# Block 2's attention as a pipeline of query tiles with a fixed TensorE order, its values in two passes, and nine of 62 filter taps taken off VectorE

## The chip, the cores and the metric

The kernel runs on 1 core of one Trainium2 chip. The metric is the device time of one execution in microseconds (us). A core has five engines that run at the same time, each through its own list of instructions in order: TensorE (PE in the profile; its weight loads are PEld), VectorE (DVE), ScalarE (ACT), GpSimd (POOL) and SyncE (SP), which here only issues DMAs.

## The reference, cut to what matters

Two transformer blocks run one after the other on a sequence of 512 tokens of width 1024, in float32. The change is inside the mixer of the second block, which sends four column groups of one projection `u = h @ w_in` through four mixers and joins them:

```python
z = val * jax.nn.sigmoid(gate)                       # conformer mixer: 256 channels
z = causal_depthwise_conv(z, dw_w) + dw_b            # 31 taps per channel
z = group_norm_channels(z, gn_g, gn_b)               # mean and variance over 64 channels
y_a = jax.nn.silu(z)
y_b = b_gate * causal_depthwise_conv(c_gate * xs, conv_w)        # short mixer, 3 taps
y_c = moba_attention(u_att)                          # 4 heads of 64, 512 keys
y_d = h_lru * jax.nn.gelu(gate)                      # RG-LRU: two small products, gates, a scan
y = jnp.concatenate([y_a, y_b, y_c, y_d], axis=-1) @ w_out[l]
```

With 512 tokens the attention is an ordinary causal softmax with a linear distance bias, four heads of width 64: scores, softmax over the keys, and the product with the values.

## The kernel before, in words

The sequence is four token tiles of 128 (`NT = 4`). A product in nearly full float32 precision is made of three passes of a faster type (`F32R`): each operand is split into a high part, copied by ScalarE, and a low part, `source - high`, by VectorE (`split`, L111 to L113), and `mm3` adds high x high, high x low and low x high in one PSUM bank. A weight column block of 1024 rows x 128 columns is eight such triples, 24 matmuls into one tile `cm` of 128 channels x 512 tokens (`cm_phase`, L156). Weights come by SP's DMA queue into `rawc`/`rawr`, and ScalarE and VectorE split them into `wh` and `wl`, five buffers of each (`WB = 5`).

The program is written for a tile framework that schedules it: each engine's order is set by the framework's own timeline, not by the order of the Python code alone. So in the kernel before, matmuls of the attention and of the projections may change places on TensorE.

Block 2's mixer, in the order of the code. First the conformer's gate and value blocks give `zp` (a padded 128 x 542 tile for each half of the 256 channels). The filter is 62 VectorE steps, 31 for each half, into `cacc0` and `cacc1` (`taps`, L1125): one `tensor_scalar` and 30 `scalar_tensor_tensor` each. They wait in a list `bg`, and `pump(n)` takes the next n of them into the program at chosen places, `RATE = 5` behind each column block. Then come the attention's query and key blocks (`aq_evac`, `ak_evac`), and the value block in token layout (`tm_block`, tile `tmc`, evacuated to `av` in plain float32).

Then the four heads follow one after another. `at_head(h)` makes four query tiles of scores (`as`, two passes), adds the bias and takes the row minimum on VectorE (L1192, tile `aL`), the exponential with its row sum on ScalarE (L1194), the reciprocal and the scaling on VectorE (L1195, L1196), and the transposes on TensorE (`apt`, L1199), which ScalarE and VectorE copy in turn to `apts` (L1200). Four float32 value products follow (`ao`, L1250). Behind each head come two or three of nine more column blocks (`rest`: gate, RG-LRU input, short mixer), and behind the first two heads one half of the RG-LRU (`lru`, tiles `lps`, `xc`). Behind head 2 all remaining taps are put in and the group norm begins (`conf_mean`, tile `cmu`); behind head 3 it ends (`conf_norm`, tile `cva`).

PSUM has eight banks: three for `cm`, `lps`, `cmu` and `cva` in rotation (`mm`), two for scores (`s`), two for transposes (`pt`), one for the value product (`o`). The output projection of the mixer follows (`tm_phase` with `order4 = [6, 7, 2, 3, 4, 5, 0, 1]`, tile `tm`, L223 to L227): it takes the RG-LRU's chunks first, then the short mixer's (2, 3), the attention's (4, 5) and the conformer's (0, 1).

Of the kernel before, what the change touches and what calls it, by code (L numbers as in the profile page):

```python
# [8 lines left out]
F32 = mybir.dt.float32  # L9
F32R = mybir.dt.float32r  # L10
AF = mybir.ActivationFunctionType
OP = mybir.AluOpType
# [3 lines left out]
P = 128  # L16
T = 512
NT = T // P
D = 1024
KC = D // P  # L20
# [6 lines left out]
NEG = -1.0e30  # L27
# [14 lines left out]
def tile_two_blocks(ctx: ExitStack, tc: tile.TileContext, a: dict, out: bass.AP, dbg=None):  # L42
# [39 lines left out]
    ident = consts.tile([P, P], F32, name="ident")  # L82
# [69 lines left out]
    def pump(n):  # L152
        for _ in range(min(n, len(bg))):
            bg.pop(0)()
# [881 lines left out]
    for g in range(2):  # L1036
        pool.memset(gmean[64 * g:64 * g + 64, 64 * g:64 * g + 64], 1.0 / 64.0)
    def tmp():
        return mx.tile([P, T], F32, name="tmp", tag="tmp", bufs=6)

    zp = [mx.tile([P, 30 + T], F32, name=f"zp{c}") for c in range(2)]
    th_g = {}
# [38 lines left out]
    cs, cx = {}, {}  # L1081

    def sc_c(c):
        def f(ps):
            cs[c], cx[c] = tmp(), tmp()
            act.activation(cs[c], ps, AF.Copy)
        return f

    def sc_x(c):
        def f(ps):  # L1090
            dve.tensor_mul(cx[c], cs[c], ps)
            w = pv[:, c, SCW:SCW + 3]
            act.activation(cs[c], cx[c], AF.Copy, scale=w[:, 2:3])
            for j in (1, 0):
                s = 2 - j
                dve.scalar_tensor_tensor(cs[c][:, s:], cx[c][:, :T - s], w[:, j:j + 1], cs[c][:, s:],
                                         op0=OP.mult, op1=OP.add)
        return f

    def sc_b(c):  # L1100
        def f(ps):
            dve.tensor_mul(cx[c], cs[c], ps)
            split(H3[0][:, 2 + c, :], H3[1][:, 2 + c, :], cx[c])
        return f

    gl = {}
# [15 lines left out]
    lg = col_blocks(w_in2, 2304, 256)  # L1122
    acc = [mx.tile([P, T], F32, name=f"cacc{c}") for c in range(2)]

    def taps(c):  # L1125
        z, w = zp[c], half[:, c, :]
        bg.append(lambda: dve.tensor_scalar(acc[c], z[:, 0:T], w[:, 0:1], pv[:, c, DWB:DWB + 1],
                                            op0=OP.mult, op1=OP.add))
        for j in range(1, 31):
            bg.append(lambda j=j: dve.scalar_tensor_tensor(acc[c], z[:, j:j + T], w[:, j:j + 1], acc[c],  # L1130
                                                           op0=OP.mult, op1=OP.add))

    sq, var = {}, {}

    def conf_mean():
        for c in (1, 0):
# [45 lines left out]
    def at_head(h):  # L1182
        pts = m2.tile([P, NT, T], F32, name="apts", tag="apts", bufs=1)
        for i in range(NT):
            n = (i + 1) * P
            s = psm.tile([P, T], F32, name="as", tag="s", bufs=2)
            m = max(n, 256)
            for j in range(2):
                pe.matmul(s[:, :m], aq(h)[:, i * P:(i + 1) * P], ak(h)[j][:, :m], start=j == 0, stop=j == 1)
            L = m2.tile([P, T], F32, name="aL", tag="aL", bufs=2)  # L1190
            st = m2.tile([P, 3], F32, name="ast", tag="ast", bufs=4)
            dve.tensor_tensor_reduce(L[:, :n], s[:, :n], ab[:, T - n:], scale=-0.25 ** (h + 1), scalar=-NEG,  # L1192
                                     op0=OP.add, op1=OP.min, accum_out=st[:, 0:1])
            act.activation(L[:, :n], L[:, :n], AF.Exp, scale=-1.0, bias=st[:, 0:1], accum_out=st[:, 1:2])  # L1194
            dve.reciprocal(st[:, 2:3], st[:, 1:2])  # L1195
            dve.tensor_scalar(L[:, :n], L[:, :n], st[:, 2:3], None, op0=OP.mult)  # L1196
            pt = psm.tile([P, NT, P], F32, name="apt", tag="pt", bufs=2)
            for kb in range(i + 1):
                pe.transpose(pt[:, kb, :], L[:, kb * P:(kb + 1) * P], ident)  # L1199
            (act.copy if i % 2 else dve.tensor_copy)(pts[:, 0:i + 1, i * P:(i + 1) * P], pt[:, 0:i + 1, :])  # L1200
        return pts
# [4 lines left out]
    for c in (1, 0):  # L1206
        taps(c)
    dump("x3", X)
    lnp.release()
    psm = Banks(mm=(0, 1, 2), s=(3, 4), pt=(5, 6), o=(7,))  # L1210
# [10 lines left out]
    akp = m2.tile([P, 2, 2, T], F32R, name="akp")  # L1221

    def aq(h):
        return H3[h % 2][:, 4 + h // 2, :]

    def ak(h):
        return [H3[i][:, h, :] if h < 2 else akp[:, h - 2, i, :] for i in range(2)]

    av = m2.tile([P, NT, 256], F32, name="av")
# [8 lines left out]
    rest = chunks[5:]  # L1238
    for c in range(2):
        rest += [(sc[c], sc_c(c)), (sx[c], sc_x(c)), (sb[c], sc_b(c))]  # L1240
    cuts = (0, 3, 4, 6, len(rest))


    for c in range(2):
        o = psm.tile([P, T], F32, name="ao", tag="o", bufs=1)
        for e in range(2):
            h = 2 * c + e
            pts = at_head(h)
            for kb in range(NT):
                pe.matmul(o[64 * e:64 * e + 64, kb * P:], av[:, kb, h * 64:(h + 1) * 64], pts[:, kb, kb * P:],  # L1250
                          start=kb == 0, stop=kb == NT - 1)
            cm_phase(*MM, rest[cuts[h]:cuts[h + 1]], X3, 0, rate=RATE)
            if h in (0, 1):
                lru(h)
            if h == 2:
                pump(len(bg))
                conf_mean()
            if h == 3:
                conf_norm()
        split(H3[0][:, 4 + c, :], H3[1][:, 4 + c, :], o)  # L1260
    dump("h3h", H3[0].bitcast(F32))
    m2.release()
    mx.release()
# [145 lines left out]
```

## Time and profile before

| | before |
|---|---|
| median of 3 runs | 1320.06 us (1317.81 to 1320.11) |
| the profiled execution, its own time | 1320.28 us |
| its span, first to last instruction | 1318.6 us |
| mean granted TensorE clock | 0.994 |
| TensorE busy | 1302.3 us, 99% |
| VectorE busy | 744.4 us, 56% |
| ScalarE busy | 533.9 us, 40% |
| GpSimd busy | 75.8 us, 6% |

The profiled execution's own time lies 0.2 us above the median, and 1.7 us of it lie outside the span. The mixer's part that the change touches runs from about 785 to 925 us of the span. Times in rows are counted from the span's start. A matmul's listed duration includes its way through the array, so the time that one takes from the next is read from start to start.

### The profile page before, as it was taken

What the parts mean: (1) busy time and instruction counts of PE and PEld (TensorE: products, weight loads), DVE (VectorE), ACT (ScalarE), POOL (GpSimd) and SP (SyncE); (2) the same over time, 40 slices, a digit from 0 to 9 for tenths busy, and PEclk for the clock granted to TensorE, in tenths of its full rate; (3) what the DMA queues carried; (4) which work ended last, traced back from release to release, by engine and by line L of the source; (5) the groups of instructions that cost most, each with busy time, mean ns of one, the idle gap of its engine ahead of it and who ended that gap; (6) DMA issues with size and microseconds to landing.
All of it is one profiled execution on the core that took longest, in us unless ns stands there. A gap on an engine that the chain in (4) does not pass through costs nothing.

```text
span 1318.6 us, 17034 instructions
## 1 busy us (share of the span) xinstructions
PE 1302.3 (99%) x6906; PEld 1115.0 (85%) x6906; DVE 744.4 (56%) x1203; ACT 533.9 (40%) x893; POOL 75.8 (6%) x152
## 2 busy tenths in 40 slices
PE   9999999999999999999999999999999999999998
PEld 8899899899889888888888898767898888888886
DVE  6764876574666655556633569985553334532432
ACT  5764564333423433344432134665433223431321
POOL 3220020110010000000000120000100000000000
PEclk9999999998999999999999999989999999999999
DMA  8322344522223342323233024212324332223211
GB/s 267 97 67 71 112 138 158 200 90 99 94 96 130 111 128 65 127 68 124 82 110 128 32 69 147 73 37 64 99 95 128 96 96 97 96 96 112 96 37 59
DMA packets 92148, 134.87 MB, mean 102 GB/s; under 512 B 4572, under 2 KB 77329, under 8 KB 92062
## 3 DMA queue, kind: packets, MB, share of 16 engines
q1 hardware_dynamic: 88446, 128.53, 29.9%
q10 hardware_dynamic: 2968, 3.14, 0.7%
q0 software_dynamic: 656, 2.12, 0.5%
q8 instruction: 54, 0.88, 0.3%
q14 instruction: 24, 0.20, 0.0%
HBM read 131.66 MB, written 2.12 MB: 101 GB/s over the span
## 4 chain that ended last, share of the span: by engine, by line
PE 94%; DVE 3%; ACT 2%; issue 0%; DMA 0%; POOL 0%; ACTq 0%; DVEq 0%; POOLq 0%
PE cm L139 15%; PE cm L138 15%; PE cm L140 15%; PE tm L227 9%; PE tm L223 9%; PE tm L224 9%; PE tmc L200 2%; PE tmc L201 2%; PE tmc L199 2%; PE tr L294 1%; PE tm L138 1%; PE tm L140 1%; PE tm L139 1%; PE num L687 1%; DVE cacc L1130 1%; PE mls L667 1%
## 5 line engine op out<-in xcount | busy, mean ns | idle before, releaser
L113 DVE TENSOR_TENSOR wl<-rawc,wh 128x1024 fp32r<-128x1024 f32 x140 | 170.7, 1222 | 203.2 <-ACT wh L112 202.9
L112 ACT ACTIVATE wh<-rawc 128x1024 fp32r<-128x1024 f32 x140 | 147.7, 1058 | 224.9 <-PE cm L139 190.6
L113 DVE TENSOR_TENSOR wl<-rawr,wh 128x1024 fp32r<-128x1024 f32 x73 | 88.9, 1223 | 147.1 <-ACT wh L112 147.1
L112 ACT ACTIVATE wh<-rawr 128x1024 fp32r<-128x1024 f32 x73 | 76.9, 1060 | 174.6 <-PE tm L227 126.5
L139 PE MATMUL cm<-x2l,wh 128*128 128x512 f32 (+1 forms) x392 | 143.8, 368 | 0.0
L140 PE MATMUL cm<-x2h,wl 128*128 128x512 f32 (+1 forms) x392 | 143.7, 367 | 0.0
L138 PE MATMUL cm<-x2h,wh 128*128 128x512 f32 (+1 forms) x392 | 143.1, 368 | 0.0
L139 PE MATMUL cm<-x4l,wh 128*128 128x512 f32 (+1 forms) x296 | 106.6, 361 | 1.3 <-DVE x4l L113 1.3
L140 PE MATMUL cm<-x4h,wl 128*128 128x512 f32 (+1 forms) x296 | 106.4, 360 | 0.0
L138 PE MATMUL cm<-x4h,wh 128*128 128x512 f32 (+1 forms) x296 | 106.1, 361 | 0.1
L139 PEld LDWEIGHTS cm<-x2l,wh 128*128 128x128 f32 x392 | 73.9, 189 | 12.2
L140 PEld LDWEIGHTS cm<-x2h,wl 128*128 128x128 f32 x392 | 73.8, 189 | 12.1
L138 PEld LDWEIGHTS cm<-x2h,wh 128*128 128x128 f32 x392 | 73.6, 189 | 12.2
L631 DVE SCALAR_TENSOR_TENSOR uy<-cm,fw,uy 128x511 f32<-128x511 f32 x88 | 65.5, 747 | 1.4
L138 PE MATMUL cm<-x3h,wh 128*128 128x512 f32 (+1 forms) x184 | 64.2, 354 | 0.8 <-DVE xc L631 0.6
L139 PE MATMUL cm<-x3l,wh 128*128 128x512 f32 (+1 forms) x184 | 64.5, 351 | 0.0
L139 PEld LDWEIGHTS cm<-x4l,wh 128*128 128x128 f32 x296 | 55.8, 189 | 9.8 <-DVE x4l L113 1.5
L140 PE MATMUL cm<-x3h,wl 128*128 128x512 f32 (+1 forms) x184 | 63.9, 349 | 0.0
L138 PEld LDWEIGHTS cm<-x4h,wh 128*128 128x128 f32 x296 | 55.5, 189 | 8.9 <-DVE x4l L113 0.3
L140 PEld LDWEIGHTS cm<-x4h,wl 128*128 128x128 f32 x296 | 55.8, 189 | 8.5
L329 POOL TENSOR_TENSOR rs_r<-rs_e,mhalf 128x1 f32<-128x1 f32 (+1 forms) x16 | 24.2, 1510 | 540.6 <-DVE rs_e L328 540.6
L200 PE MATMUL tmc<-wl,xh 128*128 128x256 f32 (+1 forms) x160 | 46.5, 290 | 0.7 <-DVE wl L113 0.7
(460 smaller groups left out, 3053.1 us busy)
## 6 DMA issues: line engine op xcount, KB each, us to landing
rawc<-in_ffn_w_up_dram SPq DMA_DIRECT2D x22, 1024.0 KB
rawc<-in_w_in_dram SPq DMA_DIRECT2D x20, 1024.0 KB
rawc<-in_mlp_w_dram SPq DMA_DIRECT2D x16, 1024.0 KB
rawr<-in_mlp_w_dram SPq DMA_DIRECT2D x16, 1024.0 KB
rawr<-in_ffn_w_down_dram SPq DMA_DIRECT2D x11, 1024.0 KB
rawr<-in_w_out_dram SPq DMA_DIRECT2D x10, 1024.0 KB
rawc<-in_xa_wkv_dram SPq DMA_DIRECT2D x8, 1024.0 KB
rawc<-in_xa_wq_dram SPq DMA_DIRECT2D x4, 1024.0 KB
```

What stands on the lines that cost most here:

```text
L112: act.activation(hi, src, AF.Copy)
L113: dve.tensor_sub(lo, src, hi.bitcast(F32))
L138: pe.matmul(ps, wh, xh, start=first, stop=False)
L139: pe.matmul(ps, wh, xl, start=False, stop=False)
L140: pe.matmul(ps, wl, xh, start=False, stop=last)
L199: pe.matmul(o, xh, wh, start=k == 0, stop=False)
L200: pe.matmul(o, xh, wl, start=False, stop=False)
L201: pe.matmul(o, xl, wh, start=False, stop=k == KC - 1)
L223: pe.matmul(ps[t][h], xh, wh[:, c], start=i == 0, stop=False)
L224: pe.matmul(ps[t][h], xh, wl[:, c], start=False, stop=False)
L227: pe.matmul(ps[t][h], xl, wh[:, c], start=False, stop=i == n - 1)
L631: dve.scalar_tensor_tensor(dst[:, s:], ps[:, :T - s], w[:, j:j + 1], y[:, s:], op0=OP.mult, op1=OP.add)
```

## The change

Six things change, all in block 2's mixer.

1. The attention runs as one pipeline over 16 units (four heads x four query tiles). Step u issues the scores of unit u, then 12 or 15 matmuls of the nine column blocks (a generator, `stream`), then the transposes of unit u - 2, and in every second step the value product of a pair of query tiles, whose second tile was transposed one step before.
2. These matmuls and transposes are wrapped in `in_order`, which keeps them on TensorE in the order of the code. The other engines are still scheduled by the framework.
3. The values are split (`av`: 64 high and 64 low columns side by side), the transposed probabilities are split too (`ptp`), and the value product is two passes of 256 columns per key block; the high and low output halves are added afterwards (`aos`). The scaling by the reciprocal sum goes from VectorE to ScalarE.
4. Of the second half's 31 taps, nine go to ScalarE: the first writes `cacc1`, eight write a scaled copy `ctap` (two buffers), and a DMA on GpSimd's queue adds each to `cacc1`. They are spaced by `next_act_tap` at nine places. VectorE's 22 other taps of that half start when the last add has landed.
5. The background list holds all of half 0, then half 1, and is taken out 4 steps behind a query or key block, 6 behind a half of the value block, then 1 or 2 in each step of the pipeline.
6. One square in `lru` goes from VectorE to ScalarE, the order of the two halves in the group norm changes, and it stands behind the whole attention.

```diff
+    in_order = tc.keep_in_program_order
...
-    def taps(c):
-        z, w = zp[c], half[:, c, :]
-        bg.append(lambda: dve.tensor_scalar(acc[c], z[:, 0:T], w[:, 0:1], pv[:, c, DWB:DWB + 1],
-                                            op0=OP.mult, op1=OP.add))
-        for j in range(1, 31):
...
+    NDMA = 8
+
+    def act_tap(j):
+        z, w = zp[1], half[:, 1, :]
+        if j == 0:
+            act.activation(acc[1], z[:, 0:T], AF.Identity, scale=w[:, 0:1], bias=pv[:, 1, DWB:DWB + 1])
+            return
+        t = mx.tile([P, T], F32, name="ctap", tag="ctap", bufs=2)
+        in_order(act.activation(t, z[:, j:j + T], AF.Copy, scale=w[:, j:j + 1]))
+        pool.dma_start(acc[1], t, accum_op=OP.add)
...
+            for j in range(NDMA + 1 if c else 1, 31):
+                bg.append(lambda z=z, w=w, c=c, j=j: dve.scalar_tensor_tensor(
+                    acc[c], z[:, j:j + T], w[:, j:j + 1], acc[c], op0=OP.mult, op1=OP.add))
...
-        dve.tensor_mul(lps[0], av_, av_)
+        act.activation(lps[0], av_, AF.Square)
...
-        act.activation(av[:, t0:t0 + 2, :], ps.rearrange("p (u c) -> p u c", u=2), AF.Copy)
+        v = av[:, t0:t0 + 2].rearrange("p u h d -> p (u h) d")
+        split(v[:, :, 0:64], v[:, :, 64:P], ps.rearrange("p (u d) -> p u d", d=64))
         pump(RATE)
+        next_act_tap()
-    RATE = 5
+    RATE = 6
...
-    cm_phase(*MM, ATT, X3, 0, rate=RATE)
+    for chunk in ATT:
+        cm_phase(*MM, [chunk], X3, 0, rate=4)
+        next_act_tap()
...
+    def stream():
+        for n, (src, evac) in enumerate(rest):
+            w = split_w(src())
+            ps = psm.tile([P, T], F32, name="cm", tag="mm", bufs=3)
+            for k in range(KC):
+                for i, (wi, xi) in enumerate(((0, 0), (0, 1), (1, 0))):
+                    in_order(pe.matmul(ps, w[wi][:, k, :], X3[xi][:, k, :], start=k == 0 and i == 0,
+                                       stop=k == KC - 1 and i == 2))
+                if k == KC - 1:
+                    evac(ps)
+                if (n, k) in ((2, KC - 1), (3, 5)):
+                    lru(n - 2)
+                yield
...
-            dve.tensor_scalar(L[:, :n], L[:, :n], st[:, 2:3], None, op0=OP.mult)
+        act.activation(L[:, :n], L[:, :n], AF.Copy, scale=st[:, 2:3])
...
+        d = ptp[i // 2][:, :, 0:i + 1, (i % 2) * P:(i % 2 + 1) * P]
+        split(d[:, 0], d[:, 1], pt[:, 0:i + 1, :])
...
+        for kb in range(2 * p + 2):
+            for i in range(2):
+                in_order(pe.matmul(o[:, p * 256:(p + 1) * 256], av[:, kb, h, :], ptp[p][:, i, kb, :],
+                                   start=kb == 0 and i == 0, stop=kb == 2 * p + 1 and i == 1))
...
+    for u in range(N + 3):
+        if u < N:
+            at_scores(*units[u])
+        upto = min((u + 1) * len(rest) * KC // N, len(rest) * KC)
+        for _ in range(upto - done):
+            next(filler)
+        done = upto
+        if 2 <= u < N + 2:
+            at_turn(*units[u - 2])
+        if u >= 4 and u % 2 == 0:
+            at_sum(units[u - 3][0], units[u - 3][1] // 2)
+        if u in (0, 2):
+            next_act_tap()
+        pump(1 if u < 3 else 2)
```

What this does to the lists of instructions is seen at two places. On TensorE in the kernel before, around the first value product (`ao`), the rows are these; `cm` is a column block, `apt` a transpose, `as` a score, `lps` a product of the RG-LRU:

```order
L1199 MATMUL apt<-ident,aL 128x128 x4
L1189 MATMUL as<-h3h,h3l 128x256
L1189 MATMUL as<-h3l 128x256
L1189 MATMUL as<-h3h,h3l 128x256
L1189 MATMUL as<-h3l 128x256
L1250 MATMUL ao<-apts,av 64x512
L1250 MATMUL ao<-apts,av 64x384
L1250 MATMUL ao<-apts,av 64x256
L1250 MATMUL ao<-apts,av 64x128
L1189 MATMUL as<-h3h,h3l 128x384
...
L1163 MATMUL lps<-xc_6842,bd 128x512 x2
L1199 MATMUL apt<-ident,aL 128x128 x3
```

On TensorE now, at its first value product (the first pair of query tiles of head 0), with the rows of the next step behind it:

```order
L1258 MATMUL cm<-x3h,wl 128x512
L1291 MATMUL apt<-ident,aL 128x128 x3
L1301 MATMUL ao<-apts_7471,av 128x256 x4
L1277 MATMUL as<-h3h,h3l 128x256
L1277 MATMUL as<-h3l 128x256
L1258 MATMUL cm<-x3h,wh 128x512
...
L1188 MATMUL lps<-xc_6842,bd 128x512 x2
...
L1291 MATMUL apt<-ident,aL 128x128 x4
```

Before, the value products stood among scores and transposes, in four sizes; now each stands behind 12 column-block matmuls and one unit's transposes, and no later matmul of the pipeline may pass it.

On VectorE now, from the first unit's transposes (`apt_7560`) to the second's (`apt_7601`); `cacc1` is the second filter half, whose first VectorE tap this is, and L115 is the low part of a split:

```order
L115 TENSOR_TENSOR apts0_7471<-apt_7560,apts0_7471 128x128
L1283 RECIPROCAL ast_7572<-ast_7572 128x1
L115 TENSOR_TENSOR wl_7902<-rawc_7778,wh_7901 128x1024
L1155 SCALAR_TENSOR_TENSOR cacc1_6845<-zp1_6839,half_628,cacc1_6845 128x512
L1280 ISA aL_7611,ast_7612<-as_7608,ab_7158 128x128
L1280 ISA ast_7612 128x1
L633 SCALAR_TENSOR_TENSOR xc0_6842<-cm_7534,pv_623,xc0_6842 128x511
L115 TENSOR_TENSOR apts0_7471<-apt_7601,apts0_7471 128x2x128
```

On VectorE before, from the first head's first transposed tile on:

```order
L1200 COPY apts_7454<-apt_7464 128x128
L1192 ISA aL_7483,ast_7484<-as_7480,ab_7157 128x384
L1192 ISA ast_7484 128x1
L1192 ISA aL_7497,ast_7498<-as_7494,ab_7157 128x512
L1192 ISA ast_7498 128x1
L1130 SCALAR_TENSOR_TENSOR cacc1_6845<-zp1_6839,half_628,cacc1_6845 128x512
L1130 SCALAR_TENSOR_TENSOR cacc0_6844<-zp0_6838,half_628,cacc0_6844 128x512
L113 TENSOR_TENSOR wl_7870<-rawc_7867,wh_7869 128x1024
```

Before, taps of both halves were free to run from the start, and taps of both still come here. Now the taps ahead of this place are all of half 0, and the 22 of half 1 begin here, behind the last adding DMA, between the splits on which the value products wait.

## Rows read from the trace of the kernel before

**Rows 1.** The page: busy time of each engine, and the chain's shares.
```profile
PE 1302.3 (99%) x6906; PEld 1115.0 (85%) x6906; DVE 744.4 (56%) x1203; ACT 533.9 (40%) x893; POOL 75.8 (6%) x152
...
PE 94%; DVE 3%; ACT 2%; issue 0%; DMA 0%; POOL 0%; ACTq 0%; DVEq 0%; POOLq 0%
```

**Rows 2.** Stretches of block 2's mixer: length, then PE, PEld, DVE, ACT, POOL; clock; DMA.
```profile
800.00:823.00 23.00, 23.00 (x123) 19.90 (x122) 22.57 (x31) 11.75 (x17) 0.00 (x0) 1.00 0.35 111
823.00:854.00 31.00, 29.38 (x163) 24.33 (x162) 29.13 (x56) 18.44 (x31) 0.00 (x0) 1.00 0.19 62
854.00:870.00 16.00, 13.15 (x41) 8.68 (x42) 15.38 (x33) 8.92 (x14) 0.00 (x0) 0.79 0.20 67
```

**Rows 3.** TensorE's timeline in the attention: start, us, instruction, count, idle before and releaser.
```profile
817.93 0.28 PE L199 MATMUL tmc<-wh,x3h 128*128 128x256 f32 x1
...
829.80 0.28 PE L201 MATMUL tmc<-wh,x3l 128*128 128x256 f32 x1
...
850.23 2.34 PE L1250 MATMUL ao<-apts,av 128*64 128x512 f32 x8 [1.34 <-DVE apts L1200]
...
853.86 1.95 PE L1163 MATMUL lps<-xc,bd 128*128 128x512 f32 x4 [0.29 <-issue]
858.09 0.95 PE L1199 MATMUL apt<-ident,aL 128*128 128x128 f32 x3 [2.28 <-DVE aL L1196]
859.61 0.80 PE L138 MATMUL cm<-x3h,wh 128*128 128x512 f32 x1 [0.57 <-DVE xc L631]
...
872.52 0.39 PE L139 MATMUL cm<-x3l,wh 128*128 128x512 f32 x1
872.75 0.39 PE L140 MATMUL cm<-x3h,wl 128*128 128x512 f32 x1
...
919.57 2.37 PE L1250 MATMUL ao<-apts,av 128*64 128x512 f32 x8
921.87 0.50 PE L227 MATMUL tm<-wh,h3l 128*128 128x512 f32 x1
```

**Rows 4.** Single microseconds around the fall and the rise of the clock.
```profile
858.00:859.00 1.00, 0.91 (x3) 0.47 (x3) 1.00 (x4) 0.08 (x1) 0.00 (x0) 0.55 0.00 0
...
864.00:865.00 1.00, 1.00 (x4) 0.76 (x3) 1.00 (x4) 0.99 (x2) 0.00 (x0) 0.53 0.00 0
865.00:866.00 1.00, 1.00 (x6) 0.82 (x5) 1.00 (x3) 0.56 (x1) 0.00 (x0) 1.00 0.00 0
```

**Rows 5.** VectorE's timeline, two busy pieces: start to start is an instruction's price.
```profile
850.00 1.40 DVE L1130 SCALAR_TENSOR_TENSOR cacc<-zp,half,cacc 128x512 f32<-128x512 f32 x2
851.32 0.28 DVE L1192 CUSTOM_DVE_ANT_0 aL<-as,ab 128x128 f32<-128x128 f32 x1
...
851.88 1.22 DVE L113 TENSOR_TENSOR wl<-rawc,wh 128x1024 fp32r<-128x1024 f32 x1
853.01 1.40 DVE L631 SCALAR_TENSOR_TENSOR xc<-cm,pv,xc 128x509 f32<-128x509 f32 x2
...
858.21 0.68 DVE L1176 SCALAR_TENSOR_TENSOR tmp<-tmp,xc 128x512 f32<-128x512 f32 x1
858.82 0.74 DVE L631 SCALAR_TENSOR_TENSOR xc<-cm,pv,xc 128x509 f32<-128x509 f32 x1
```

**Rows 6.** ScalarE's timeline around its function table's load and a weight copy.
```profile
825.67 1.28 ACT L1194 ACT_TABLE_LOAD   x1
826.97 0.40 ACT L1194 ACTIVATE aL<-aL,ast 128x128 f32<-128x128 f32 x1
...
842.17 1.05 ACT L112 ACTIVATE wh<-rawc 128x1024 fp32r<-128x1024 f32 x1
843.12 0.76 ACT L628 ACTIVATE xc<-cm,pv 128x512 f32<-128x512 f32 x1
```

**Rows 7.** DMA issues on GpSimd's queue: tile, size, median us from issue to landing.
```profile
swb<-vfwd_d POOLq DMA_DIRECT2D x1, 1024.0 KB, 8.9
...
mb<-mrow_d POOLq DMA_DIRECT2D x4, 256.0 KB, 3.5
```

More of the change, by code (lines that the diff above doesn't have):

```diff
@@ L1101, in f @@
         def f(ps):
-            dve.tensor_mul(cx[c], cs[c], ps)
-            split(H3[0][:, 2 + c, :], H3[1][:, 2 + c, :], cx[c])
+            dve.tensor_mul(cs[c], cs[c], ps)
+            split(H3[0][:, 2 + c, :], H3[1][:, 2 + c, :], cs[c])
         return f
@@ L1123, in tile_two_blocks, with next_act_tap, taps @@
     acc = [mx.tile([P, T], F32, name=f"cacc{c}") for c in range(2)]
-    def taps(c):
-        z, w = zp[c], half[:, c, :]
-        bg.append(lambda: dve.tensor_scalar(acc[c], z[:, 0:T], w[:, 0:1], pv[:, c, DWB:DWB + 1],
-                                            op0=OP.mult, op1=OP.add))
-        for j in range(1, 31):
-            bg.append(lambda j=j: dve.scalar_tensor_tensor(acc[c], z[:, j:j + T], w[:, j:j + 1], acc[c],
-                                                           op0=OP.mult, op1=OP.add))
+    NDMA = 8
[7 more added lines that the diff above has]
+        pool.dma_start(acc[1], t, accum_op=OP.add)
+    act_taps = iter(range(NDMA + 1))
+    def next_act_tap():
+        for j in act_taps:
+            act_tap(j)
+            return
+    def taps():
+        for c in (0, 1):
+            z, w = zp[c], half[:, c, :]
+            if c == 0:
+                bg.append(lambda z=z, w=w, c=c: dve.tensor_scalar(acc[c], z[:, 0:T], w[:, 0:1], pv[:, c, DWB:DWB + 1],
+                                                                  op0=OP.mult, op1=OP.add))
+            for j in range(NDMA + 1 if c else 1, 31):
+                bg.append(lambda z=z, w=w, c=c, j=j: dve.scalar_tensor_tensor(
+                    acc[c], z[:, j:j + T], w[:, j:j + 1], acc[c], op0=OP.mult, op1=OP.add))
     sq, var = {}, {}
     def conf_mean():
-        for c in (1, 0):
+        for c in (0, 1):
             ps = psm.tile([P, T], F32, name="cmu", tag="mm", bufs=3)
@@ L1180, in lru @@
         split(H3[0][:, 6 + c, :], H3[1][:, 6 + c, :], xc[c])
[L1182 to L1195, printed above, removed]
-            dve.tensor_scalar(L[:, :n], L[:, :n], st[:, 2:3], None, op0=OP.mult)
[L1197 to L1201, printed above, removed]
     chunks = ([(cg[c], cgate_evac(c)) for c in range(2)] + [(cv[c], cval_evac(c)) for c in range(2)]
@@ L1205, in tile_two_blocks @@
     cm_phase(psl, "mm", 8, chunks[:5], X3, SK, fin)
-    for c in (1, 0):
-        taps(c)
+    taps()
+    next_act_tap()
     dump("x3", X)
@@ L1226, in ak @@
     def ak(h):
-        return [H3[i][:, h, :] if h < 2 else akp[:, h - 2, i, :] for i in range(2)]
-    av = m2.tile([P, NT, 256], F32, name="av")
+        return [H3[i][:, h, :] for i in range(2)]
+    av = m2.tile([P, NT, 4, P], F32R, name="av")
     def av_evac(t0, ps):
-        act.activation(av[:, t0:t0 + 2, :], ps.rearrange("p (u c) -> p u c", u=2), AF.Copy)
+        v = av[:, t0:t0 + 2].rearrange("p u h d -> p (u h) d")
+        split(v[:, :, 0:64], v[:, :, 64:P], ps.rearrange("p (u d) -> p u d", d=64))
@@ L1244, in tile_two_blocks @@
[L1244 to L1260, printed above, removed]
+    rest = chunks[5:] + [(sc[0], sc_c(0)), (sx[0], sc_x(0)), (sc[1], sc_c(1)), (sx[1], sc_x(1)),
+                         (sb[0], sc_b(0)), (sb[1], sc_b(1))]
@@ new lines, in tile_two_blocks, with at_scores @@
+    filler = stream()
+    ptp = [m2.tile([P, 2, 2 * p + 2, 256], F32R, name=f"apts{p}") for p in range(2)]
+    for p in range(2):
+        pool.memset(ptp[p][:, :, 2 * p + 1, 0:P].bitcast(F32), 0.0)
+    Ls, os_, osum = {}, {}, {}
+    def at_scores(h, i):
+        n = (i + 1) * P
+        s = psm.tile([P, T], F32, name="as", tag="s", bufs=2)
+        m = max(n, 256)
+        for j in range(2):
+            in_order(pe.matmul(s[:, :m], aq(h)[:, i * P:(i + 1) * P], ak(h)[j][:, :m], start=j == 0, stop=j == 1))
+        L = m2.tile([P, T], F32, name="aL", tag="aL", bufs=3)
+        st = m2.tile([P, 3], F32, name="ast", tag="ast", bufs=4)
+        dve.tensor_tensor_reduce(L[:, :n], s[:, :n], ab[:, T - n:], scale=-0.25 ** (h + 1), scalar=-NEG,
+                                 op0=OP.add, op1=OP.min, accum_out=st[:, 0:1])
+        act.activation(L[:, :n], L[:, :n], AF.Exp, scale=-1.0, bias=st[:, 0:1], accum_out=st[:, 1:2])
+        dve.reciprocal(st[:, 2:3], st[:, 1:2])
+        act.activation(L[:, :n], L[:, :n], AF.Copy, scale=st[:, 2:3])
+        Ls[h, i] = L
@@ new lines, in at_turn, with at_sum @@
+    def at_turn(h, i):
+        L = Ls.pop((h, i))
+        pt = psm.tile([P, NT, P], F32, name="apt", tag="pt", bufs=2)
+        for kb in range(i + 1):
+            in_order(pe.transpose(pt[:, kb, :], L[:, kb * P:(kb + 1) * P], ident))
+        d = ptp[i // 2][:, :, 0:i + 1, (i % 2) * P:(i % 2 + 1) * P]
+        split(d[:, 0], d[:, 1], pt[:, 0:i + 1, :])
+    def at_sum(h, p):
+        if p == 0:
+            os_[h] = psm.tile([P, T], F32, name="ao", tag="o", bufs=1)
+        o = os_[h]
+        for kb in range(2 * p + 2):
+            for i in range(2):
+                in_order(pe.matmul(o[:, p * 256:(p + 1) * 256], av[:, kb, h, :], ptp[p][:, i, kb, :],
+                                   start=kb == 0 and i == 0, stop=kb == 2 * p + 1 and i == 1))
+        if p == 1:
+            c, e = h // 2, h % 2
+            if e == 0:
+                osum[c] = m2.tile([P, T], F32, name="aos", tag="aos", bufs=1)
+            r = osum[c][HALF[e], :]
+            act.copy(r, o[HALF[1 - e], :])
+            dve.tensor_add(r, o[HALF[e], :], r)
+            if e == 1:
+                split(H3[0][:, 4 + c, :], H3[1][:, 4 + c, :], osum[c])
@@ new lines, in tile_two_blocks @@
+    units = [(h, i) for h in range(4) for i in range(NT)]
+    N = len(units)
+    done = 0
+    for u in range(N + 3):
[10 more added lines that the diff above has]
+        if u in (0, 2):
+            next_act_tap()
+        pump(1 if u < 3 else 2)
@@ L1261, in tile_two_blocks @@
+    for _ in filler:
+        pass
+    pump(len(bg))
+    conf_mean()
+    conf_norm()
     dump("h3h", H3[0].bitcast(F32))
```

18 lines of the change are left out of this document (7 added, 11 removed).

## The prediction

> **What bounds the kernel now.** I read the page first: TensorE is busy for 99% of the span, and 94% of the chain that ended last is its own [rows 1]. So the change can gain only where TensorE waits or does work that can shrink, and it loses wherever TensorE starts to wait. The stretches of block 2's mixer come next: from 800 to 823 us TensorE has no gap and VectorE is busy for 22.57 of 23 us; from 823 to 854 TensorE has 29.38 of 31 and VectorE 29.13; from 854 to 870 TensorE has 13.15 of 16, VectorE 15.38, and the clock's mean is 0.79 [rows 2]. VectorE is as full as TensorE here. TensorE's timeline names the gaps: 1.34 us ahead of a value product, for VectorE's copy of a transposed tile; 0.29; 2.28 ahead of transposes, for VectorE's scaling; 0.57 for `xc` [rows 3]. Together 4.5 us. After the longest one the granted clock falls to 0.55, half speed, and is whole again just before 865 [rows 4]: from 858.09 to 864.89 are 6.8 us, less the 0.57 of waiting, and half of it, 3.1 us, is lost. **All that the old order loses here is 7.6 us**, 0.6% of the time.
>
> **The change part by part.** The sum is made against the profiled execution's 1320.28 us, which lies 0.2 us above the median of the runs; I put it on the median, 1320.1.
>
> *Values.* A head's float32 value products take 2.30 us, from start to start, 919.57 to 921.87 [rows 3]. Now a head has 12 matmuls of 256 columns. From 817.93 to 829.80 TensorE put out some 100 matmuls, nearly all of that width, 0.12 us each [rows 3]. So 1.44 us, 0.86 less for each of four heads: **-3.4 us**. Scores, transposes and column blocks keep their number and size.
>
> *The old gaps.* They go with the old order: **-7.6 us**, if nothing takes their place.
>
> *Adding DMAs.* No transfer in the trace adds, so its price is bounded. Each moves 256 KB inside the chip. The nearest row has the same size on the same queue, 3.5 us to landing; the far end is the 1 MB row, 8.9 us [rows 7]. An add reads the sum besides the copy, so 512 KB; on the line between the two rows that is 5.3 us. I take 4.4, midway. By the Trainium skill, "DMA: Bandwidth & Descriptors", section on the anatomy of one DMA on the GpSimd path, a transfer costs about 2.0 us and its bytes at 436 GB/s, an estimate of 2.6 us here. The 3.5 us row says more. By 2.6 no add would be late.
>
> The eight adds all write `cacc1`, so they are serial. The fourth can start when ScalarE has done the last key block, about 825.7, where its table load begins [rows 6]; five landings later, at 825.7 + 5 x 4.4 = 847.7, VectorE may begin half 1. With 3.5 it is 843.2, with 5.3 852.2.
>
> *First value product.* TensorE leaves the value block at 829.44 (829.92 less the four scores that stood inside it). To its first value product it has 66 matmuls of 512 columns at 0.23 us, as from 872.52 to 872.75 [rows 3], 15.0 us, and 16 short ones of scores and transposes, 2.3 us: it is there at 846.7. The product needs the split of the second unit's transposes, which on VectorE stands behind a weight's low part, the first tap of half 1, a score and a short-filter step. ScalarE must first make that weight's high part: from 829.5 on there are three table loads of 1.3 us, three weight copies of 0.97 [rows 6] and 13 activations between 0.2 and 0.71 us by their columns, 6.6 us: 842.9 without waits, 844.5 with some. VectorE's low part, 1.13 us [rows 5], is done at 845.7; then VectorE waits until 847.7 for the last add. Tap 0.66, score 0.2, short filter 0.66, split 0.34 [rows 5] bring 849.7. **TensorE waits 3.1 us**: 0.9 with the fastest adds (VectorE then follows ScalarE), 7.4 with 5.3.
>
> *Between the first and the third product* (head 1's first pair) VectorE has, by its new order, 18 taps at 0.66 us (11.9), five other filter steps (3.3), two low parts (2.3), one RG-LRU half with eight plain steps at 0.61 and a scan, taken like a low part (6.0), and scores, reciprocals, splits and a head's sum, some 4.1 by their columns [rows 5]: 27.6 us. TensorE has 54 column-block matmuls (12.3), four float32 products of the RG-LRU at 0.97 (3.9) [rows 3], 12 value matmuls (1.4) and 16 short ones (2.4): 20.0. Since its order is fixed and the split stands behind the taps, it waits the difference, **7.6 us**, in pieces: at `lps`, at a column block whose bank isn't evacuated yet, and at the product. To the fourth product VectorE has 8.75 us, TensorE 7.9: **0.9**. Behind it TensorE has more work than VectorE up to the end, and I put nothing.
>
> *Clock.* Waits of 2 to 3 us are as long as the one that was followed by half speed [rows 3, 4]. I put the same price once, **+3.1**; the ends are 0 and twice that.
>
> *Costed at nothing.* Scaling and a square on ScalarE: it gains some 24 us over a stretch in which it had 18.44 of 31 and 8.92 of 16 [rows 2], so it is nearly full, but it hands on one unit two steps ahead; without that cover each late scaling is TensorE's. VectorE gives up 9 taps (5.9), scalings, copies and squares (10.7 by columns) and gets splits and head sums (11.9): 5 us net, which do not count where the taps' place is what delays. The group norm's order lies behind the short pieces of the output projection. SP's transfers keep their order.
>
> Sum: -3.4 - 7.6 + 3.1 + 7.6 + 0.9 + 3.1 = **+3.7 us, 1323.8**.
>
> **The rivals.**
> *Faster.* The price of VectorE's queue is too high: it holds work between two products that the old order already did at its pace with 4.5 us of gaps, and 5 us of its work are gone. If it has its work done ahead (banks and buffers let it run before TensorE), only the gain is left: 1320.1 - 11.0 = 1309.1. The point that decides: new waits and clock together under 11.0 - 2.6 = 8.4 us. For it speaks that VectorE and TensorE were about equal from 800 to 870 [rows 2]; against it, that the new taps of half 1 cannot start before the last add. The centre of this case is 1314.
>
> *No change.* Adds land in 3.5 us and the clock stays whole: 0.9 + 7.6 + 0.9 = 9.4 of waits against 11.0: 1318.5.
>
> *The adds are far slower.* At 8.9 us the last lands at 870.2, 22.5 us later than I take, and 20 to 30 us are lost: 1345. What speaks for it is only the 1 MB row; against it the four times smaller size. Each 0.1 us in an add costs 0.5 us once an add takes over 4. A rule of the Trainium skill speaks for it: "SBUF — State Buffer", on the two sides of SBUF, says that a DMA on GpSimd's queue cannot have its descriptors written while VectorE runs a two-port copy. No row here shows such a delay.
>
> **How the numbers follow.** About 0.2%, 2.6 us, is what this kernel's measurement can tell from no change. My forecast's case, slower by 1 to 9 us, has 0.42; the adds far slower 0.06; no change 0.22; faster 0.30. From the cases: faster 0.32, same 0.21, slower 0.47, with the edges shared. The range: from 1311, most of the faster case, to 1333, the forecast with adds at 5.3 us (+4.3) and the clock's price twice (+3.1); outside lie the slow adds and the best of the faster case, under 2 in 10. The forecast's own range is 1321 to 1331.
>
> **What the profile after would show.** Value products as 256-column matmuls, 0.12 us apart. On TensorE a wait of about 3 us at the first of them, for VectorE's split, and VectorE idle just ahead of its first tap of half 1, released by a DMA. Then waits of some 7 us up to the third product, named for VectorE. A clock of about half in some stretch behind them. GpSimd's queue with eight rows of 256 KB, 4 to 5 us each. Wrong would be: TensorE without gaps from 830 to 880 (faster case); VectorE waiting for ScalarE's scaling or high parts rather than for adds; adds above 6 us. It would be wrong too if the value products cost TensorE as much as before, since then 3.4 us of the gain don't exist.

## The result: slower by 0.95%

The changed kernel takes 1332.28 us (median of 4 runs, 1330.23 to 1334.91), the kernel before 1318.98 (4 runs beside it): a ratio of 1.0095, 95% interval 1.008 to 1.011. The profiled execution spans 1330.6 us, 12.0 more than the profiled one before. The forecast was slower, 1323.8 in a range of 1311 to 1333.

The page after, the rows that answer to [rows 1]: TensorE's own work is as long as before, its share of the chain fell from 94 to 91%, and 2% are now a DMA.

```profile
PE 1300.9 (98%) x6922; PEld 1118.3 (84%) x6922; DVE 742.0 (56%) x1190; ACT 557.4 (42%) x934; POOL 82.8 (6%) x162
...
PE 91%; ACT 3%; DVE 3%; DMA 2%; issue 0%; ACTq 0%; DVEq 0%; POOLq 0%
```

The stretches of [rows 2] after, with one more, and three single microseconds that answer to [rows 4]; the columns are the same:

```profile
800.00:823.00 23.00, 23.00 (x123) 19.88 (x122) 22.04 (x29) 14.31 (x20) 2.64 (x3) 1.00 0.45 124
823.00:854.00 31.00, 24.38 (x139) 20.97 (x137) 15.19 (x29) 20.07 (x34) 4.34 (x6) 0.95 0.62 152
854.00:870.00 16.00, 9.10 (x25) 6.30 (x26) 14.49 (x28) 8.95 (x16) 0.00 (x0) 0.71 0.01 2
870.00:886.00 16.00, 13.64 (x55) 10.44 (x54) 14.56 (x27) 12.85 (x22) 0.00 (x0) 0.84 0.17 52
...
858.00:859.00 1.00, 1.00 (x5) 0.81 (x5) 1.00 (x3) 0.01 (x1) 0.00 (x0) 0.50 0.00 0
870.00:871.00 1.00, 1.00 (x7) 1.00 (x6) 0.75 (x2) 0.10 (x1) 0.00 (x0) 0.50 0.06 16
882.00:883.00 1.00, 1.00 (x4) 0.78 (x3) 1.00 (x4) 0.68 (x1) 0.00 (x0) 0.50 0.00 0
```

VectorE, full before from 823 to 854 (29.13 of 31), now works 15.19 us there. TensorE lost five microseconds in that stretch, four in the next, and the mean clock is 0.71 and 0.84 in the last two. At 858, 870 and 882 it stands at half speed: it fell not once but three times. TensorE's timeline after, all its waits from 830 to 980 and one value product:

```profile
848.22 0.38 PE L1301 MATMUL ao<-apts,av 128*128 128x256 f32 x1 [1.23 <-ACT apts L114]
856.89 1.01 PE L1301 MATMUL ao<-apts,av 128*128 128x256 f32 x3 [8.29 <-DVE apts L115]
866.92 0.47 PE L1258 MATMUL cm<-x3h,wh 128*128 128x512 f32 x1 [4.01 <-DVE xc L633]
880.68 0.50 PE L1258 MATMUL cm<-x3h,wh 128*128 128x512 f32 x1 [2.36 <-ACT tmp L1088]
...
896.38 1.20 PE L1301 MATMUL ao<-apts,av 128*128 128x256 f32 x8
897.41 0.39 PE L1277 MATMUL as<-h3h 128*128 128x512 f32 x1
...
969.88 1.06 PE L296 MATMUL tr<-ident,hx 128*128 128x128 f32 x8 [1.84 <-DVE hx L1000]
971.20 0.62 PE L140 MATMUL cm<-x4h,wh 128*128 128x256 f32 x3 [0.25 <-ACT x4h L114]
972.97 0.39 PE L141 MATMUL cm<-x4l,wh 128*128 128x256 f32 x1 [1.16 <-DVE x4l L115]
```

In the attention 15.9 us of waits stand where 4.5 stood [rows 3]; the first value product alone waits 9.5. The reason stands in three other queues. These are the timelines after of VectorE (around its first tap of half 1), of GpSimd (the adds from the third on) and of SyncE (its 1 MB weight loads from 821 on):

```profile
846.66 1.22 DVE L115 TENSOR_TENSOR wl<-rawc,wh 128x1024 fp32r<-128x1024 f32 x1 [0.79 <-ACT wh L114]
854.89 0.75 DVE L1155 SCALAR_TENSOR_TENSOR cacc<-zp,half,cacc 128x512 f32<-128x512 f32 x1 [7.00 <-DMA cacc<-ctap]
...
856.43 0.41 DVE L115 TENSOR_TENSOR apts<-apt,apts 128x256 fp32r<-128x256 f32 x1
...
822.19 0.85 POOL L1139 DMA_DIRECT2D cacc<-ctap  x1 [8.30 <-ACT ctap L1138]
829.35 0.86 POOL L1139 DMA_DIRECT2D cacc<-ctap  x1 [6.30 <-DMA cacc<-ctap]
833.17 0.86 POOL L1139 DMA_DIRECT2D cacc<-ctap  x1 [2.96 <-DMA cacc<-ctap]
837.01 0.85 POOL L1139 DMA_DIRECT2D cacc<-ctap  x1 [2.98 <-DMA cacc<-ctap]
840.85 0.86 POOL L1139 DMA_DIRECT2D cacc<-ctap  x1 [2.98 <-DMA cacc<-ctap]
847.83 0.86 POOL L1139 DMA_DIRECT2D cacc<-ctap  x1 [6.12 <-ACT aL L1284]
...
821.75 0.37 SPq L105 DMA_DIRECT2D rawc<-in_w_in_dram  x1
...
840.31 7.97 SPq L110 DMA_DIRECT2D rawr<-in_w_out_dram  x2
```

For 7.0 us VectorE stands at that tap, and the split that the value product needs (`apts` at 856.43) is queued behind it. From issue to landing the eight adds take 3.4, 3.3, 6.6, 3.3, 3.3, 3.3, 6.5 and 7.0 us. The three long ones are the third, seventh and eighth, each issued within 0.6 us of a weight load (821.75, 840.31, and the second of that pair at 847.9); the fourth to the seventh follow one another after 3.8 us. ScalarE's last scaled copy was ready at 844.97. The ScalarE name in the last add's row is only the latest of several waits: the seventh add landed at about 847.4, half a microsecond before the eighth starts, the same step as between the adds ahead of it. So the last one lands at 854.9.

The five other kernels below that keep these adds show the same. Of all 48 adds, the eleven issued within 0.6 us of a 1 MB load took 6.5 to 7.4 us; the nineteen with no such load issued from 3.7 us before them until they landed took 3.2 or 3.3; the rest took 3.3 to 6.3.

### The profile page after: what moved, and what is told of

It reads as the page before. It is cut to its first block, busy times and chain, and to the rows that moved or that the text cites. A ratio compares the mean times of both kernels' runs of the same rounds, so it can differ in the third digit from the quotient of the medians.

```text
span 1330.6 us, 17102 instructions
## 1 busy us (share of the span) xinstructions
PE 1300.9 (98%) x6922; PEld 1118.3 (84%) x6922; DVE 742.0 (56%) x1190; ACT 557.4 (42%) x934; POOL 82.8 (6%) x162
## 4 chain that ended last, share of the span: by engine, by line
PE 91%; ACT 3%; DVE 3%; DMA 2%; issue 0%; ACTq 0%; DVEq 0%; POOLq 0%
PE cm L141 14%; PE cm L140 14%; PE cm L142 14%; PE tm L225 9%; PE tm L226 9%; PE tm L229 9%; PE cm L1258 3%; PE tmc L202 2%; PE tmc L203 2%; PE tmc L201 2%; DMA cacc<-ctap 2%; PE tr L296 1%; PE tm L140 1%; PE tm L142 1%; PE tm L141 1%; ACT wh L114 1%
## 5 line engine op out<-in xcount | busy, mean ns | idle before, releaser
L115 DVE TENSOR_TENSOR wl<-rawc,wh 128x1024 fp32r<-128x1024 f32 x140 | 170.6, 1221 | 206.9 <-ACT wh L114 206.7
L115 DVE TENSOR_TENSOR wl<-rawr,wh 128x1024 fp32r<-128x1024 f32 x73 | 88.9, 1222 | 148.5 <-ACT wh L114 148.5
L201 PE MATMUL tmc<-wh,xh 128*128 128x256 f32 (+1 forms) x160 | 46.4, 290 | 0.7 <-ACT wh L114 0.7
L203 PE MATMUL tmc<-wh,xl 128*128 128x256 f32 (+1 forms) x160 | 46.1, 288 | 0.0
L1155 DVE SCALAR_TENSOR_TENSOR cacc<-zp,half,cacc 128x512 f32<-128x512 f32 x52 | 38.7, 745 | 7.7 <-DMA cacc<-ctap 7.0
```

What stands on the lines that cost most here:

```text
L201: pe.matmul(o, xh, wh, start=k == 0, stop=False)
L203: pe.matmul(o, xl, wh, start=False, stop=k == KC - 1)
```

## The experiments

Four ideas were at stake. Theory A: the late last add makes the loss. Rivals: B, VectorE has too much work; C, ScalarE is late; later D, the banks of PSUM. "Pinned" below means held by `in_order`, "free" means left to the framework.

**No adds.** All 31 taps of half 1 on VectorE:

```diff
-    act_taps = iter(range(NDMA + 1))
+    act_taps = iter(())
...
-            for j in range(NDMA + 1 if c else 1, 31):
+            for j in range(1, 31):
```

> All 31 taps of half 1 are VectorE's again and there are no adding DMAs; the rest is the changed kernel (1332.3 us against 1319.0 before). Theory A (TensorE's waits of 1.2, 8.3, 4.0 and 2.4 us and the half clock behind them come from VectorE's wait of 7.0 us for the last add, whose landing was doubled to 7.0 us by weight loads): VectorE was busy for only 15.2 of the 31 us from 823 to 854, nine taps are 5.9 us, so it has room; the wait for a DMA is gone and TensorE waits less than 3 us in all: 1309 to 1315. Rival B (VectorE simply has more work than TensorE between the first and the third value product, 27.6 against 20.0 us, adds or no adds): with 5.9 us more on VectorE the waits stay or grow: 1330 to 1338.

Measured: 1323.79 us against 1318.21, ratio 1.0038 (1.0024 to 1.0052). Neither range was met. The adds are worth 8.5 us between the two medians, 7.7 when each is set against the kernel before that ran beside it, but 10.1 us of waits in the attention stay:

```profile
846.47 0.62 PE L1301 MATMUL ao<-apts,av 128*128 128x256 f32 x3 [1.01 <-DVE apts L115]
851.30 3.29 PE L1188 MATMUL lps<-xc,bd 128*128 128x512 f32 x4 [2.61 <-DVE xc L633]
858.47 0.60 PE L1258 MATMUL cm<-x3h,wh 128*128 128x512 f32 x1 [3.88 <-DVE xc L633]
872.42 0.79 PE L1258 MATMUL cm<-x3h,wh 128*128 128x512 f32 x1 [2.60 <-ACT tmp L1088]
```

**A sum of their own.** The adds stay, but VectorE's taps don't wait for them:

```diff
-        pool.dma_start(acc[1], t, accum_op=OP.add)
+        pool.dma_start(accd, t, accum_op=OP.add)
...
+    dve.tensor_add(acc[1], acc[1], accd)
```

(and one buffer of `ctap` instead of two; ScalarE's first tap writes `accd`, VectorE's first one starts `cacc1`)

> The nine taps of ScalarE and the eight adding DMAs stay, but they sum into a tile of their own, which VectorE adds to the filter sum at the end (0.6 us more on VectorE); so VectorE's 22 taps of half 1 wait for no DMA. One ctap buffer instead of two. Theory A: no VectorE wait for a DMA, TensorE waits less than 3 us in all, 1308 to 1314, and a little under the kernel without adds, if VectorE's 5.9 us count at all. Rival B: the work between the first and third product stays 27.6 us, so about 7 us of waits and the half clock stay: 1322 to 1330.

Measured: 1323.37 us, ratio 1.0030 (1.0018 to 1.0042); waits of 1.06, 1.26, 4.58 and 2.13 us in the attention. The time is that without adds. So it was the wait for the last add that cost these 8 to 9 us; the same adds, when nothing waits, cost nothing here, and nine taps less on VectorE bring nothing. Theory A's range was missed all the same, and rival B's was met, in the time and in the 6.7 us of waits behind `lps`: the wait for the add is only a part of the loss.

**Earlier adds.** Two scaled copies behind each query and key block:

```diff
         cm_phase(*MM, [chunk], X3, 0, rate=4)
         next_act_tap()
+        next_act_tap()
```

> Two of ScalarE's taps instead of one behind each query and key block, so the same eight adds into the same sum, begun earlier and closer together: at 3.8 us each from 806 on, and 3.5 us more for each that meets a weight load, the last lands at 838 to 846 instead of 854.9. Theory A: VectorE's taps of half 1 start about 10 us sooner, and TensorE's first wait of 8.3 us falls to under 2; in all 1309 to 1318. Rival B: 1326 to 1333, since all the work between the two products stays.

Measured: 1330.57 us, ratio 1.0083 (1.0065 to 1.0101), outside theory A's range and inside rival B's. The last add landed 12 us sooner, at 842.6, but the framework then put nine taps of half 1 ahead of the same splits; VectorE still stood 3.07 us for the add, earlier, and the scores behind it came late for ScalarE: TensorE waits 1.21, 1.00, 3.17, 1.32, 4.01 and 2.99 us. So it doesn't isolate the landing, and decides nothing between the two.

**Taps later.** Adds as they are, VectorE's 22 taps pinned behind the first splits:

```diff
-        pump(1 if u < 3 else 2)
+        pump(1 if u < 3 else 0 if u < 6 else 2)
-        split(d[:, 0], d[:, 1], pt[:, 0:i + 1, :])
+        act.activation(d[:, 0], pt[:, 0:i + 1, :], AF.Copy)
+        in_order(dve.tensor_sub(d[:, 1], pt[:, 0:i + 1, :], d[:, 0].bitcast(F32)))
```

(and `in_order` around each of these taps)

> Adds as in the changed kernel, but VectorE's 22 taps of half 1 are pinned behind the splits of the fifth and later units (they begin behind the second value product), so no split that a value product needs stands behind the last add. Theory A and rival B both expect that TensorE's waits up to the third product go: VectorE has 18 taps or 11.9 us less there, 15.7 against 20.0 us: 1309 to 1315; A says the 7.0 us wait of VectorE for a DMA vanishes or hides. Rival C (ScalarE is the late one: it got the scaling, a square, nine taps and two more table loads, some 24 us, and hands on late): the waits stay at 5 us or more and name ScalarE: 1318 or more.

Measured: 1331.88 us, ratio 1.0094 (1.0077 to 1.0111). Theories A and B gave 1309 to 1315 and missed; rival C's range, 1318 or more, was met. The first value product now waits 2.0 us instead of 9.5, as A says, and the output projection's last matmul starts at 957.4 instead of 967.4. But the filter ends late and the time is lost again behind it. B fell here: VectorE is busy for only 9.96 of the 16 us from 854 to 870, and the waits at the column blocks are still there.

```profile
856.38 0.47 PE L1258 MATMUL cm<-x3h,wh 128*128 128x512 f32 x1 [2.98 <-DVE xc L633]
870.89 0.79 PE L1258 MATMUL cm<-x3h,wh 128*128 128x512 f32 x1 [4.69 <-ACT tmp L1088]
...
967.19 1.94 PE L296 MATMUL tr<-ident,hx 128*128 128x128 f32 x8 [6.89 <-DVE ssv L989]
```

C isn't refuted by it: the second wait names ScalarE, as do 1.5 of the 2.0 us at the first value product. But the places are telling: both are the column block behind an `lps` pair. That gave theory D.

**The RG-LRU last**, on the kernel without adds, with the output projection in the order 2, 3, 4, 5, 6, 7, 0, 1:

```diff
-                if (n, k) in ((2, KC - 1), (3, 5)):
-                    lru(n - 2)
+                if (n, k) in ((8, 7), (9, 7)):
+                    lru(int((n, k) == (9, 7)))
...
     for _ in filler:
         pass
+    lru(1)
...
-    order4 = [6, 7, 2, 3, 4, 5, 0, 1]
+    order4 = [2, 3, 4, 5, 6, 7, 0, 1]
```

> The kernel without adds (1323.8 us), and both halves of the RG-LRU stand behind all nine column blocks; the output projection takes their chunks third instead of first. Without adds TensorE still waits 2.6 us at lps, 3.9 and 2.6 us at the next two column blocks. Theory D (of the three banks that column blocks rotate through, each RG-LRU half takes two, so the block behind it gets the bank of the block just ended and stands for that block's whole evacuation): with the RG-LRU out of the stream these waits of 9.1 us go, and with them most of the half clock (some 4 us): 1310 to 1316. Rival B (VectorE, busy for 29.8 of 31 us, and ScalarE cannot keep up in this stretch wherever the RG-LRU stands): the waits come back at other blocks, or at the output projection, which then waits for the late RG-LRU: 1320 to 1328.

Measured: 1324.06 us, ratio 1.0032 (1.0022 to 1.0042). D is right on the place: in the attention only two waits of 1.0 us are left, and the last matmul of the output projection starts at 948.97 instead of 959.12. The time doesn't follow, though. It lies in rival B's range, but the waits stand at the normalization behind the output projection, not where B put them:

```profile
849.75 0.62 PE L1301 MATMUL ao<-apts,av 128*128 128x256 f32 x3 [1.00 <-DVE apts L115]
858.84 1.09 PE L1301 MATMUL ao<-apts,av 128*128 128x256 f32 x7 [1.03 <-DVE apts L115]
953.52 1.94 PE L296 MATMUL tr<-ident,hx 128*128 128x128 f32 x8 [3.94 <-DVE ssv L989]
961.60 1.94 PE L296 MATMUL tr<-ident,hx 128*128 128x128 f32 x8 [6.14 <-DVE ssv L989]
```

The filter's chunks come at 931.7 (the last `h3l` on VectorE, 931.04 and 0.69 long), when TensorE has done nearly all else; the four token tiles then end within a few microseconds, ScalarE starts on the first (`art`, 945.04) 4 us before the last matmul starts where it had 18 without adds (941.23 against 959.12), and the normalization of each tile, which the next tile's matmuls used to hide, stands bare: 10.1 us, and 3.0 more by the clock behind.

**Order left free.** `in_order` does nothing, on the changed kernel and on the one without adds:

```diff
-    in_order = tc.keep_in_program_order
+    in_order = lambda x: x
```

> The changed kernel (1332.3 us) with TensorE's order left to the framework, adds and all else as they are. Theory A: the last add still lands at about 855 us and VectorE still waits some 7 us for it, since VectorE's order has the tap ahead of the splits; TensorE can fill part of it with other column blocks: 1322 to 1330. If the order alone made the loss, 1312 to 1320.

> The kernel without adds (1323.8 us), with TensorE's order left to the framework instead of pinned. Theory D says that pinning makes each bank wait stand, since nothing may be put in its place: free, the scheduler fills them with transposes, scores and other blocks: 1312 to 1320. If pinning costs nothing (the framework's own order waits as much): 1322 to 1326.

Measured: with the adds 1328.38 us, ratio 1.0071 (1.0054 to 1.0088); without, 1317.88, ratio 0.9993 (0.9982 to 1.0004), as theory D expected. The pinned order costs 5.9 us without the adds. So two steps lead from 1332.3 back to the kernel before: the adds out (8.5 us) and the order free (5.9). Free and without adds, the longest of TensorE's waits in the attention is 1.8 us; but all of them together are 4.5 us and the half clock behind them costs 3.3, against 4.5 and 3.1 before. The old gaps have moved, they are not gone.

With the adds the comparison is not clean, though the time is in theory A's range. `in_order` is not only around matmuls and transposes: it also holds ScalarE's eight scaled copies. Freed, these come earlier: the first add starts at 796.36 instead of 807.31, and the last lands at 840.6, not at about 855 as expected; VectorE still stands 3.89 us for it instead of 7.00. TensorE waits 0.84, 0.51 and 2.73 us for low parts of queries and keys (`h3l`), where neither the changed kernel nor the free one without adds waits. So the 3.9 us by which it is faster than the changed kernel are two changes in one, and so are the 10.5 us that the adds cost in the free order.

**One bank at a time**, pinned and free: without adds, the eight products of RG-LRU and group norm issued singly, as generators stepped at chosen places of the stream; `lps[1]` instead of `lps[0]` holds the square:

```diff
+    plan = {(2, 7): ['l0'], (3, 5): ['l0'], (4, 5): ['l1'], (5, 5): ['l1'],
+            (6, 1): ['m'], (6, 7): ['m'], (7, 5): ['v'], (8, 3): ['v']}
+    steps = {"l0": lru(0), "l1": lru(1), "m": conf_mean(), "v": conf_norm()}
...
-                if (n, k) in ((2, KC - 1), (3, 5)):
-                    lru(n - 2)
+                for g in plan.get((n, k), ()):
+                    next(steps[g], None)
```

> The kernel without adds (1323.8 us), TensorE's order pinned, with the RG-LRU's four products (lps) and the group norm's four products (cmu, cva) put one at a time between column blocks, at places where the bank that each takes, and the bank that the next block takes, were freed at least half a block before; the group norm so begins in block 7 instead of behind the attention. Theory D (bank rotation makes the waits of 2.6, 3.9 and 2.6 us): they go or fall under 2 us together, the clock stays whole, and the filter's end is early enough to leave the output projection its cover, which the kernel with the RG-LRU last lacked: 1308 to 1313, faster than the kernel before (1319). Rival B (VectorE and ScalarE cannot keep up): waits of 6 us or more remain at value products and blocks: 1317 to 1324.

> The same with TensorE's order left to the framework. If the pinned order only hurt through the bank waits (theory D), freeing it now gains nothing: within 3 us of the pinned one, 1309 to 1315. If pinning costs by itself, as the 6 us between the pinned and the free kernel without adds could also mean, it is 4 us or more faster than the pinned one.

Measured: pinned 1335.19 us, ratio 1.0117 (1.0101 to 1.0134), far outside every range given; free 1316.58, ratio 0.9979 (0.9969 to 0.9990), the fastest of all and a little faster than the kernel before. In the pinned one the products themselves now wait:

```profile
855.73 1.12 PE L1195 MATMUL lps<-xc,bd 128*128 128x512 f32 x2 [2.59 <-DVE xc L633]
875.41 2.08 PE L1195 MATMUL lps<-xc,bd 128*128 128x512 f32 x2 [3.69 <-ACT tmp L1088]
893.74 1.37 PE L1166 MATMUL cmu<-cacc,gmean 128*128 128x512 f32 x2 [2.17 <-DVE tmp L1206]
896.98 2.08 PE L1166 MATMUL cmu<-cacc,gmean 128*128 128x512 f32 x2 [1.87 <-ACT tmp L1088]
```

My "freed half a block before" was counted in TensorE's work; ScalarE and VectorE had not evacuated by then (`tmp L1088` is the copy of the short mixer's block). Freed, the same program waits 0.8 us at its first `lps` and nowhere at the others. Pinning costs 18.6 us here. Since the pinned one still stands for late evacuations, this doesn't show that pinning costs by anything else.

**Adds and values in the free, spread kernel.** First the adds with a sum of their own (the diff of above), then float32 value products:

```diff
-            for i in range(2):
-                in_order(pe.matmul(o[:, p * 256:(p + 1) * 256], av[:, kb, h, :], ptp[p][:, i, kb, :], ...
+            in_order(pe.matmul(o[HALF[e], p * 256:(p + 1) * 256], av[:, kb, h * 64:(h + 1) * 64], ptp[p][:, kb, :], ...
```

> The free, spread kernel without adds (1316.6 us), with ScalarE's nine taps and the eight adding DMAs back, summed in a tile of their own so that no tap waits for them; VectorE adds it at the end of the filter. If only the wait for the last add made the adds dear, and VectorE's load is not what TensorE waits for, this is within 2 us of 1316.6. If VectorE's 5.3 us count, it is 2 us or more faster: 1311 to 1314. If the adds cost by themselves (weight loads doubled beside them, ScalarE later), 3 us or more slower: 1320 or more.

> The free, spread kernel without adds (1316.6 us), with float32 value products (six of 256 columns for each head). From 2.30 us for 1280 columns in the kernel before they cost 2.76 us for 1536 columns, against 1.44 for the two passes: 5.3 us more on TensorE for four heads; VectorE has some 8 us less. If my term for the values holds on TensorE: 1320 to 1323. If VectorE's load decides: 1316 or less.

Measured: with the adds 1323.21 us, ratio 1.0022 (1.0010 to 1.0034), 6.6 slower; with float32 1321.50, ratio 1.0011 (0.9998 to 1.0024), 4.9 slower, as expected. On the pinned kernel without adds the float32 values gave 1330.53, ratio 1.0076 (1.0058 to 1.0095), 6.7 slower, more than either theory had it:

> The kernel without adds (1323.8 us), with the value products in float32 as before: plain copies instead of splits, one float32 product per key block, no sum of two halves. TensorE's value products cost 3 to 4 us more if my term of -3.4 for the two passes holds. VectorE loses some 8 us of splits and sums, ScalarE some. Theory D (bank rotation) and the term: 1324 to 1328. Rival B (VectorE's load makes the waits): it gains more from the lighter VectorE than TensorE loses: 1317 to 1322.

Rival B fell again: 8 us less for VectorE gained nothing. What the adds cost in the free kernel, where no tap waits for them, isn't settled: TensorE's value block begins 3.0 us later (820.55 against 817.52) and has two waits of 0.64 and 1.33 us for the low parts of queries and keys (`h3l`), behind ScalarE's scaled copies, which are free here and begin earlier (the first add at 798.14), or in an order that the framework chose otherwise.

## Why the prediction came out as it did

The direction was right, by the wait at the first value product; the size was not, 3.7 us forecast and 13.3 measured (12.0 between the two profiled executions, from which the terms below are read). That the result lies within the range is in part luck: the forecast with the two additions named for its upper end is 1331.2, not 1333, and the measured time, 1332.3, lies between the two.

*Values, -3.4.* From 896.38 to 897.41 eight products take 1.03 us, and four take 0.55 (888.59 to 889.14): 1.58 for a head instead of 1.44, so 4 x (2.30 - 1.58) = -2.9. Right, and float32 again costs 4.9 in the free, spread kernel.

*The old gaps, -7.6.* They went as said: neither the copy nor the scaling on VectorE is waited for. But other waits took their place, and in the free order without adds they are as large as the old ones.

*Adding DMAs, 4.4 us each.* **This is the term that failed.** An add alone takes 3.3 us and the next follows after 3.8, but 6.5 to 7.0 beside a 1 MB load; I had taken one price for all and looked at no collision, though the change adds 2 MB of transfers to a stretch whose weight loads the trace showed. The fourth could start only at 829.35, since the third had met a load; five adds then took 25.5 us, and the last landed at 854.9, not 847.7. The rest of the chain was as walked: TensorE was there at 847.0 (forecast 846.7), VectorE's low part was done at 847.8 (845.7). The wait was 9.5 instead of 3.1 (2.9 by the prediction's own pieces). Adds above 6 us were among its signs of being wrong, and three of eight were. That the wait for the add decides is shown (its own sum: -8.9 us); that an add beside a load takes twice as long is read from 48 adds in six traces; no run moved the loads alone. The descriptor rule of the Trainium skill, "SBUF — State Buffer", section on the two sides of SBUF, doesn't explain the slowest add: VectorE stood idle from 847.9 to 854.9, for all of it, and so ran no copy that could have held it back.

*Between the first and the third product, 7.6, and 0.9 behind.* Measured 4.0 and 2.4, and nothing behind: 6.4 instead of 8.5. The size was near for a wrong reason. I set VectorE's work against TensorE's; with 11.9 us of it taken away ("Taps later"), 3.0 and 4.7 us still stand. What they wait for is the evacuation of the block just ended, and they vanish with the RG-LRU out of the stream. That three banks of which `lps` takes two are the cause fits this, and fits the free order, in which other work steps in; a version with a fourth bank wasn't tried. Why the evacuation comes late is open too, since that run also takes the RG-LRU's work away from ahead of it. In the changed kernel the second wait ends like this in the chain that ended last:

```profile
874.59 0.69 ACT tmp L1190
...
879.06 0.95 ACT wh L114
880.03 0.60 ACT tmp L1088
880.68 4.53 PE cm L1258 x12
```

ScalarE works without a gap from 874.59, the RG-LRU's pieces first and the block's copy (L1088) last. So a part of rival C stands: the block's evacuation is queued behind other work of ScalarE. Load alone is not enough, as the free order without adds has that load and no such wait; no run made only ScalarE's work lighter there. (The pinned run with float32 values, which takes work off both ScalarE and VectorE, waits 1.56 us there instead of 2.60.)

*Clock, +3.1.* I counted one fall and there were three, each in a long wait or just behind it. Their worth, TensorE's busy time times the missing share of the clock in single microseconds, summed from 845 to 905: 5.7 us, against 3.1 in the kernel before.

*Costed at nothing: behind the third product.* 1.9 us more of waits at the transposes and first products of the next stage (3.25 against 1.35). That they come from the later end of the filter is not shown.

The sum: -2.9 - 7.6 + 15.9 + 5.7 + 1.9 = +13.0, against the 12.0 between the profiled executions; one microsecond of it is unexplained. Of the rivals the slow adds came nearest in the mechanism: some 7 us, but for three of eight. The faster one named the right point, that new waits and clock stay under 8.4 us. The program that comes nearest to it has no adds, a free order and its small products spread: 1316.6, 0.2% under the kernel before, where the rival's centre was 1314.

## What to carry to other kernels

Price a transfer that something waits for beside the transfers that run at that moment, not alone, and ask what is queued behind the instruction that waits for it. Pinning an engine's order makes each late evacuation stand at its place; here it cost 6 to 19 us against the same program left free, so try the free order first and pin only what it gets wrong. When a stall moves out of a stage, look at the next stage's cover: here an output projection that ended 10 us sooner gained nothing, since the time came back at the normalization.

## What was not expected of the hardware

An adding DMA of 256 KB inside the chip took 3.3 us, no more than the plain 256 KB row of the trace before (3.5). The prediction had priced 512 KB for it, for reading the sum besides the copy; the trace counts 0.52 MB for two adds (830 to 837 us). Beside a 1 MB load an add took up to 7.0 us here, and up to 7.4 in the other kernels with adds.
